# The first FFN's down products with activations stationary, their results turned by VectorE and exchanged by DMA

## The chip, the cores and the metric

The kernel runs on one core of one Trainium2 chip. The metric is the device time of one execution in microseconds (us), as the median of several runs. TensorE does the matrix products, VectorE and ScalarE the elementwise work, GpSimd next to nothing here, and SyncE (SP) issues the DMAs that bring the weights from HBM into SBUF.

## The reference

One layer of a decoder trunk over 256 tokens of width 2048, in float32. Three sublayers each normalise x, shift and scale it by vectors computed from a conditioning vector c (adaLN), and add a gated result:

```python
c_act = silu(c)
sh1, sc1, g1, sh2, sc2, g2, sh3, sc3, g3 = split(c_act @ w_ada + b_ada, 9)
h = rms_norm(x) * (1 + sc1) + sh1
x = x + 0.5 * g1 * ((silu(h @ w1_gate) * (h @ w1_up)) @ w1_down)     # first FFN, hidden width 5632
h = rms_norm(x) * (1 + sc2) + sh2
x = x + g2 * (hybrid_mixer(h) @ w_out)                               # attention and a short convolution
h = rms_norm(x) * (1 + sc3) + sh3
x = x + 0.5 * g3 * ((silu(h @ w2_gate) * (h @ w2_up)) @ w2_down)     # second FFN
```

## The kernel before

**Precision.** Every float32 operand of a large product is split into a high part in TensorE's rounded float32 format and the remainder as a low part. A product is high x high, high x low and low x high. ScalarE makes the high part of a weight (L382), VectorE the low part (L388), right after the weight has landed.

**Entries, halves, ticks.** All weights pass one list of entries, worked off by `run`. An entry is 512 rows by 512 columns (1 MB), loaded by one DMA on SP's queue into one of five raw buffers; the load of the entry four ahead is issued at the start of an entry, so it waits for the buffer of the entry just finished. An entry is consumed in two halves of 256 rows. Four halves are split ahead of the one that TensorE multiplies (`AHEAD`), with five buffers each for high and low parts. After each half the kernel counts one tick; `at(n, fn)` lets `fn` run n ticks after the next one, which puts follow-up work at a chosen place of the instruction streams. Between the FFN's entries stand adaLN entries: 256 or 512 rows of w_ada, multiplied by c and summed by VectorE (L173), one step per 128 rows, summed over partitions at the end.

**Layouts.** x is kept transposed (`xT`: channels on partitions, tokens along the row), as is the normalised input `hS` with its high and low parts. The gate and up products use the activations as stationary operand (`mm_N`: L535, L536, L537): the result has tokens on partitions, and TensorE turns it back with identity matmuls (`flip_split`, L547) into `act`, hidden channels on partitions.

**The down products of the first FFN** use the weights as stationary operand (`group_T`, `mm_T`: L425 and L427). Per 128 rows and 128 output channels one matmul streams 512 columns (256 tokens of high and 256 of low parts) and one 256 columns. The hidden width is done in two groups of channels (six and five blocks of 512); in each, four blocks of 512 output channels, `dg` 0 to 3. A block's results are in four PSUM banks, channels on partitions; `residual` copies them out by ScalarE (L515) and adds them, times the gate, into `xT` by VectorE (L715). After the second group each finished pair of channel blocks is squared for the next norm (`after_residual`). The last 256 channels go by `mm_D` and `fin_one`, straight into the norm.

**The down products of the second FFN** use the activations as stationary operand (`group_R`, again `mm_N`): per 128 rows and 128 tokens three matmuls of 512 columns, results with tokens on partitions, two banks per block.

**The start.** Shift and scale of the first sublayer are needed before anything else, so w_ada comes in eight chunks of 256 channels of each (`ada_chunk`), and the gate and up products of the first FFN run in windows over 256 channels as these become known (`start`, `windows`). A chunk has 16 row blocks, one L173 step each; then eight passes over a matrix of ones (L239) sum over partitions and VectorE and ScalarE make the next part of `hS` (L604, L612, L615). For chunk 0 the row blocks 3, 7 and 11 (`PE_KS`) go to TensorE instead, as one-column matmuls (also L239; a float32 matmul shows as two passes in the trace). The first norm's sums of squares are made by Square on ScalarE and a reduction on VectorE (`first_norm`).

Of the kernel before, what the change touches and what calls it, by code (L numbers as in the profile page):

```python
# [10 lines left out]
F32 = mybir.dt.float32  # L11
# [5 lines left out]
P = 128  # L17
# [19 lines left out]
ATT0 = 4  # L37
QP = 4
ST = 2
DB, DQ, DS, DL, DT = 1, 1, 0, 0, 0  # L40
GT = 3
XT, XD = 8, 3
# [1 line left out]
LAG = 0  # L44
CB = 2
CW = CB * P
PE_KS = (3, 7, 11)
KEEP = 2
LAST = (0, 1, 4, 5, 2, 3, 6, 7, 10, 8, 9)
SET_A = (0, 1, 2, 3, 10)  # L50
# [4 lines left out]
class Kern:  # L55
    def __init__(self, ctx, tc, x, c, w_ada, b_ada, w1_gu, w1_down, w_in, q_norm_w, k_norm_w,
                 conv_w, w_out, w2_gu, w2_down, out):
        self.tc, self.nc = tc, tc.nc
        self.x, self.c, self.out = x[0], c, out[0]
        self.w_ada, self.b_ada = w_ada[0], b_ada  # L60
        self.w1_gu, self.w1_down, self.w2_gu, self.w2_down = w1_gu[0], w1_down[0], w2_gu[0], w2_down[0]
        self.w_in, self.w_out = w_in[0], w_out[0]
        self.qn_w, self.kn_w, self.conv_w = q_norm_w, k_norm_w, conv_w[0]
        pool = lambda name, bufs, **kw: ctx.enter_context(tc.tile_pool(name=name, bufs=bufs, **kw))
        self.const = pool("const", 1)
        self.big = pool("big", 6)
        self.rawp = pool("rawp", NRAW)
        self.hip = pool("hip", AHEAD + 1)
        self.lop = pool("lop", AHEAD + 1)
        self.adap = pool("adap", 1)  # L70
        self.ev = pool("ev", 2)
        self.gatep = pool("gatep", 2)
        self.t2 = pool("t2", NT2)
        self.small = pool("small", 2)
        self.dram = pool("dram", 2, space=bass.MemoryType.DRAM)
        self.psA = pool("psA", 6, space=bass.MemoryType.PSUM)
        self.psM = pool("psM", 2, space=bass.MemoryType.PSUM)
        self.n = 0
        self.later = deque()
        self.soft = deque()  # L80
        self.have = set()
        self.gates = {}
# [148 lines left out]
    def ada_chunk(self, ch):  # L231

        nc = self.nc
        st = {}
        direct = PE_KS if ch == 0 else ()

        def on_pe(w, one, first, last):
            for j in range(4):
# [3 lines left out]
        def make(r):  # L242
            def fn(raw):
                if r == 0:
                    if ch == 0:
                        self.ada_acc = self.adap.tile([P, 2, 512], F32, tag="ada", name=self.nm("ada"))
                    st["acc"] = self.ada_acc[:, ch % 2, :]
                for a in range(4):
                    k = 4 * r + a
                    if k not in direct:  # L250
                        self.soft.append(lambda a=a, k=k: self.ada_step(st["acc"], raw[:, a, :], k))
                for k in range(4 * r, 4 * r + 4):
                    if k in direct:
                        if k == direct[0]:
                            st["ps"] = self.misc()
                        on_pe(raw[:, k % 4, :], self.cact[:, k:k + 1], k == direct[0], False)
            return fn

        def parts(r):
            return lambda raw: [(raw[:, :, CW * s:CW * (s + 1)],  # L260
# [5 lines left out]
        def end():  # L266
            while self.soft:
                self.soft.popleft()()
            if not direct:
                st["ps"] = self.misc()  # L270
            on_pe(st["acc"], self.ones[:, 0:1], not direct, True)
# [257 lines left out]
    def mm_N(self, acc, hi, lo, h, first, last, tts=(0, 1)):  # L529

        nc = self.nc
        for tt in tts:
            ts = slice(tt * P, (tt + 1) * P)
            for kk in range(2):
# [2 lines left out]
                nc.tensor.matmul(acc[tt], h[kk][:, 1, ts], hi[:, kk, :], start=False, stop=last and kk == 1,  # L537
                                 skip_group_check=True)

    def flip_split(self, dst, src):  # L540

        nc = self.nc
# [93 lines left out]
    def first_norm(self):  # L636
# [3 lines left out]
        sq = self.bigt(F32).rearrange("p a b t -> p (a b t)")  # L640
        for i in range(4):
            part = sq[:, 1024 * (i % 2):1024 * (i % 2 + 1)]
            nc.scalar.activation(part, self.xs[i // 2][:, 1024 * (i % 2):1024 * (i % 2 + 1)], AF.Square)
            nc.vector.reduce_sum(self.ssx[:, i:i + 1], part, axis=AX.X)

        def flip(ks, tiles):
            for tt in range(2):
# [55 lines left out]
    def residual_rows(self, dg, tt, acc):  # L703
# [55 lines left out]
    def ffn(self, w_gu, w_down, gate, done, done_last, first):  # L759
# [4 lines left out]
        rows = [512 * u for u in range(4)]  # L764
        act, sil = {}, {}

        def fin_gate(cg):
            def fin(acc):
                sil[cg] = [self.tmp()[:, 0:512] for _ in range(2)]
                for tt in range(2):  # L770
                    nc.scalar.activation(sil[cg][tt], acc[tt], AF.Silu)
            return fin

        def fin_up(cg):
            def fin(acc):
                act[cg] = self.bigt()
                for tt in range(2):
                    nc.vector.tensor_mul(sil[cg][tt], acc[tt], sil[cg][tt])
                self.at(ST, lambda: self.flip_split(act[cg], sil[cg]))
            return fin  # L780

        rhs = lambda k: self.hS[:, k]
# [16 lines left out]
        for gi, (a, b) in enumerate(GROUPS):  # L799
# [6 lines left out]
            for dg in range(4):  # L806
# [392 lines left out]
```

## Time and profile before

| | |
|---|---|
| Median of 3 runs | 1918.27 us (1916.52 to 1919.71) |
| Profiled execution, own time | 1920.87 us |
| Its span | 1919.2 us |
| TensorE busy | 1887.4 us, 98% |
| VectorE busy | 1408.9 us, 73% |
| ScalarE busy | 928.5 us, 48% |
| DMA | 501.79 MB, mean 261 GB/s |

The profile is of one execution. The span runs from the first to the last instruction; what lies around it makes up the difference to the execution's own time. Matmuls are pipelined, so the recorded durations of neighbours overlap, and the distance between starts tells what one costs.

### The profile page before, as it was taken

The numbers are of one execution on the slowest core, as the hardware profiler recorded it, in microseconds if no ns is written. First come the engines' busy times: TensorE is split into PE (matmuls) and PEld (weight loads), VectorE is DVE, ScalarE is ACT, GpSimd is POOL, SyncE is SP. The second block draws the span as 40 slices with busy tenths as digits, with TensorE's granted clock in tenths as the row PEclk, the third lists the DMA queues.
The fourth block names the chain that finished last, engine by engine and source line by source line (L and its number), as shares of the span: only waits on it lengthen the run. The fifth ranks groups of instructions, "written<-read, shape, count | busy, mean of one in ns | idle before, by whom it ended". The sixth has DMA issues, their size and how long they took to land.

```text
span 1919.2 us, 23244 instructions
## 1 busy us (share of the span) xinstructions
PE 1887.4 (98%) x9127; PEld 1585.5 (83%) x9127; DVE 1408.9 (73%) x1614; ACT 928.5 (48%) x1167; POOL 2.0 (0%) x11
## 2 busy tenths in 40 slices
PE   5999999999999999999999999999999999999998
PEld 4888888888888888888888888888888888888887
DVE  7878888788788789787889997667675545554454
ACT  4667784444444444456554454544443334444432
POOL 0000000000000000000000000000000000000000
PEclk8999999999999999999999999999999999999999
DMA  9898988888888878678769885677775556555562
GB/s 363 308 328 311 335 284 307 303 286 324 297 305 310 314 274 313 214 260 284 264 231 328 296 314 190 202 263 269 283 266 210 197 197 197 184 189 193 180 212 73
DMA packets 240678, 501.79 MB, mean 261 GB/s; under 512 B 8430, under 2 KB 43448, under 8 KB 240312
## 3 DMA queue, kind: packets, MB, share of 16 engines
q1 hardware_dynamic: 240536, 500.30, 74.4%
q8 instruction: 71, 1.16, 0.2%
q14 instruction: 39, 0.32, 0.0%
q10 hardware_dynamic: 32, 0.01, 0.0%
HBM read 498.17 MB, written 2.11 MB: 261 GB/s over the span
## 4 chain that ended last, share of the span: by engine, by line
PE 97%; DVE 2%; DMA 1%; ACT 0%; issue 0%; SPq 0%; DVEq 0%
PE acc L535 23%; PE acc L536 23%; PE acc L537 23%; PE acc L425 16%; PE acc L427 8%; DVE ada L173 1%; PE m L547 1%; DMA raw<-in_w_ada_dram 1%; PE acc L437 0%; PE acc L438 0%; PE acc L436 0%; DVE lo L388 0%; PE m L239 0%; PE m L1084 0%; PE m L1061 0%
## 5 line engine op out<-in xcount | busy, mean ns | idle before, releaser
L388 DVE TENSOR_TENSOR lo<-raw,hi 128x1024 fp32r<-128x1024 f32 x656 | 792.6, 1222 | 399.8 <-ACT hi L382 396.6
L382 ACT CAST hi<-raw 128x1024 fp32r<-128x1024 f32 x656 | 685.1, 1052 | 736.5 <-PE acc L537 493.5
L535 PE MATMUL acc<-hi,hS 128*128 128x512 f32 x1600 | 632.5, 395 | 7.3 <-ACT hS L612 7.2
L536 PE MATMUL acc<-lo,hS 128*128 128x512 f32 x1600 | 626.7, 392 | 1.3 <-DVE lo L388 1.3
L537 PE MATMUL acc<-hi,hS 128*128 128x512 f32 x1600 | 626.5, 392 | 0.0
L173 DVE SCALAR_TENSOR_TENSOR ada<-raw,cact,ada 128x1024 f32<-128x1024 f32 (+1 forms) x327 | 357.1, 1092 | 8.4 <-DMA raw<-in_w_ada_dram 1.4
L535 PEld LDWEIGHTS acc<-hi,hS 128*128 128x128 f32 x1600 | 302.8, 189 | 70.1 <-ACT hS L612 8.1
L536 PEld LDWEIGHTS acc<-lo,hS 128*128 128x128 f32 x1600 | 303.0, 189 | 63.6 <-DVE lo L388 2.3
L537 PEld LDWEIGHTS acc<-hi,hS 128*128 128x128 f32 x1600 | 302.5, 189 | 64.1 <-DVE hS L615 0.4
L425 PE MATMUL acc<-big,hi 128*128 128x512 f32 x888 | 315.4, 399 | 0.0
L427 PE MATMUL acc<-big,lo 128*128 128x256 f32 x888 | 249.5, 281 | 0.0
L425 PEld LDWEIGHTS acc<-big,hi 128*128 128x128 f32 x888 | 166.9, 188 | 40.5
L427 PEld LDWEIGHTS acc<-big,lo 128*128 128x128 f32 x888 | 167.9, 189 | 0.1
L535 PE MATMUL acc<-hi,big 128*128 128x512 f32 x352 | 137.2, 390 | 0.0
L536 PE MATMUL acc<-lo,big 128*128 128x512 f32 x352 | 137.0, 389 | 0.0
L537 PE MATMUL acc<-hi,big 128*128 128x512 f32 x352 | 137.0, 389 | 0.0
L425 PE MATMUL acc<-hS,hi 128*128 128x512 f32 x384 | 136.5, 400 | 0.0
L427 PE MATMUL acc<-hS,lo 128*128 128x256 f32 x384 | 107.3, 279 | 0.0
L425 PEld LDWEIGHTS acc<-hS,hi 128*128 128x128 f32 x384 | 72.2, 188 | 16.8
L536 PEld LDWEIGHTS acc<-lo,big 128*128 128x128 f32 x352 | 66.1, 188 | 13.7
L535 PEld LDWEIGHTS acc<-hi,big 128*128 128x128 f32 x352 | 66.1, 188 | 13.7
L537 PEld LDWEIGHTS acc<-hi,big 128*128 128x128 f32 x352 | 66.1, 188 | 13.7
(151 smaller groups left out, 910.6 us busy)
## 6 DMA issues: line engine op xcount, KB each, us to landing
raw<-in_w_gu_dram SPq DMA_DIRECT2D x170, 1024.0 KB, 5.2
raw<-in_w_ada_dram SPq DMA_DIRECT2D x112, 1024.0 KB, 5.2
raw<-in_w_down_dram SPq DMA_DIRECT2D x88, 1024.0 KB, 5.6
raw<-in_w_in_dram SPq DMA_DIRECT2D x48, 1024.0 KB, 7.2
raw<-in_w_ada_dram SPq DMA_DIRECT2D x64, 512.0 KB, 5.6
raw<-in_w_out_dram SPq DMA_DIRECT2D x16, 1024.0 KB, 6.1
raw<-in_w_gu_dram SPq DMA_DIRECT2D x12, 512.0 KB, 5.5
big<-in_x_dram SPq DMA_DIRECT2D x2, 1024.0 KB, 7.0
```

Source lines behind the costliest of these rows:

```text
L173: nc.vector.scalar_tensor_tensor(acc, w, self.cact[:, k:k + 1], acc, op0=ALU.mult, op1=ALU.add)
L382: nc.scalar.copy(hi, raw[:, 2 * h:2 * h + 2, :])
L388: nc.vector.tensor_sub(lo, raw[:, 2 * h:2 * h + 2, :], hi.bitcast(F32))
L425: nc.tensor.matmul(o, hi[:, kk, cs], rhs[kk].rearrange("p a t -> p (a t)"), start=first and kk == 0, stop=False)
L427: nc.tensor.matmul(o[:, 0:T], lo[:, kk, cs], rhs[kk][:, 0, :], start=False, stop=last and kk == 1)
L535: nc.tensor.matmul(acc[tt], h[kk][:, 0, ts], hi[:, kk, :], start=first and kk == 0, stop=False, skip_group_check=True)
L536: nc.tensor.matmul(acc[tt], h[kk][:, 0, ts], lo[:, kk, :], start=False, stop=False, skip_group_check=True)
L537: nc.tensor.matmul(acc[tt], h[kk][:, 1, ts], hi[:, kk, :], start=False, stop=last and kk == 1, skip_group_check=True)
L547: nc.tensor.transpose(ps[:, i * T + tt * P:i * T + (tt + 1) * P], src[tt][:, (2 * pr + i) * P:(2 * pr + i + 1) * P], self.ident)
```

## The change

The down products of the first FFN, except the last 512 output channels after the second group, use `group_R`: activations stationary, results with tokens on partitions in two PSUM banks. `turned` brings them back: VectorE transposes each bank in blocks of 32 x 32 from PSUM into an SBUF tile with the blocks in another order; four ticks after the next one, 16 DMAs on SP's queue, each 32 partitions x 2 x 128 values (32 KB), carry the blocks to their partitions; three ticks later four VectorE operations multiply by the gate and add into `xT`. A pool for one exchanged tile is new. There is also a path that would treat the activations in the same way; `on_pe` returns True always, so it isn't taken.

Two more edits are at the start. `PE_KS` now sends row blocks 3, 7, 11 and 15 of chunk 0 and row blocks 13, 14 and 15 of chunk 1 to TensorE; those of chunk 1 are multiplied when the chunk ends. And the first norm's reduction on VectorE is replaced by the sum that ScalarE's Square can give along with its result.

```diff
+SX, SA = 4, 7
-PE_KS = (3, 7, 11)
+PE_KS = {0: (3, 7, 11, 15), 1: (13, 14, 15)}
+        self.exp = pool("exp", 1)
 ...
-        direct = PE_KS if ch == 0 else ()
+        direct = PE_KS.get(ch, ())
 ...
+                if ch == 0:
+                    rows_on_pe(r, raw)
+                elif r == 3:
+                    st["raw"] = raw
 ...
+        def rows_on_pe(r, raw):
+            for k in range(4 * r, 4 * r + 4):
+                if k in direct:
+                    if k == direct[0]:
+                        st["ps"] = self.misc()
+                    on_pe(raw[:, k % 4, :], self.cact[:, k:k + 1], k == direct[0], False)
 ...
         def end():
             while self.soft:
                 self.soft.popleft()()
+            if ch:
+                rows_on_pe(3, st["raw"])
 ...
+    def exchange(self, tr, fn):
+        st = {}
+        def go():
+            ex = self.exp.tile([P, 2, 512], F32, tag="ex", name=self.nm("ex"))
+            for a in range(4):
+                for c in range(4):
+                    self.nc.sync.dma_start(ex[32 * c:32 * c + 32, :, P * a:P * (a + 1)],
+                                           tr[32 * a:32 * a + 32, :, P * c:P * (c + 1)])
+            st["ex"] = ex.rearrange("p tt (a k j) -> p k (tt a) j", a=4, k=4)
+        self.at(SX, go)
+        self.at(SA, lambda: fn(st["ex"]))
 ...
-            nc.scalar.activation(part, self.xs[i // 2][...], AF.Square)
-            nc.vector.reduce_sum(self.ssx[:, i:i + 1], part, axis=AX.X)
+            nc.scalar.activation(part, self.xs[i // 2][...], AF.Square,
+                                 accum_out=self.ssx[:, i:i + 1])
 ...
+    def turned(self, dg, gate, done):
+        st = {}
+        def add(ex):
+            for k in range(4):
+                d = 4 * dg + k
+                self.want(gate, d // 8)
+                xd = self.xT[:, d, :].rearrange("p (ta j) -> p ta j", j=32)
+                self.nc.vector.scalar_tensor_tensor(xd, ex[:, k], self.mod[:, 16 * gate + d:16 * gate + d + 1], xd,
+                                                    op0=ALU.mult, op1=ALU.add)
+                if done and k % 2:
+                    done(d - 1)
+        def finish(tt, acc):
+            if tt == 0:
+                st["tr"] = self.ev.tile([P, 2, 512], F32, tag="ev", name=self.nm("ev"))
+            self.nc.vector.transpose(st["tr"][:, tt, :].rearrange("p (c k j) -> p c k j", k=4, c=4), self.by_quad(acc))
+            if tt == 1:
+                self.exchange(st["tr"], add)
+        return finish
 ...
-                if first:
-                    down += self.group_T(w_down, urows, 512 * dg, lhs, fin, fin_one if last and dg == 3 else None)
+                if not first:
+                    down += self.group_R(w_down, urows, 512 * dg, lhs, fin_rows)
+                elif last and dg == 3:
+                    down += self.group_T(w_down, urows, 512 * dg, lhs, fin, fin_one)
                 else:
-                    down += self.group_R(w_down, urows, 512 * dg, lhs, fin_rows)
+                    down += self.group_R(w_down, urows, 512 * dg, lhs, self.turned(dg, gate, done if last else None))
```

## Rows read from the trace of the kernel before

**Rows 1.** The page: busy time of the engines; the chain that ended last.

```profile
PE 1887.4 (98%) x9127; PEld 1585.5 (83%) x9127; DVE 1408.9 (73%) x1614; ACT 928.5 (48%) x1167; POOL 2.0 (0%) x11
...
PE 97%; DVE 2%; DMA 1%; ACT 0%; issue 0%; SPq 0%; DVEq 0%
```

**Rows 2.** Timeline of ScalarE, first FFN's down products: start, us, instruction [idle before <-releaser].

```profile
352.44 1.05 ACT L382 CAST hi<-raw 128x1024 fp32r<-128x1024 f32 x1 [1.78 <-PE acc L425]
...
375.04 1.05 ACT L382 CAST hi<-raw 128x1024 fp32r<-128x1024 f32 x1 [1.77 <-PE acc L425]
```

**Rows 3.** Windows: length, busy of PE, PEld, DVE, ACT, POOL, PEclk, DMA share, GB/s.

```profile
311.60:448.50 136.90, 136.90 (x781) 118.99 (x780) 108.08 (x121) 57.01 (x63) 0.00 (x0) 1.00 0.85 302
674.00:787.00 113.00, 113.00 (x684) 100.20 (x683) 91.92 (x117) 50.96 (x62) 0.00 (x0) 1.00 0.81 286
```

**Rows 4.** Timeline of TensorE, the start.

```profile
19.75 1.71 PE L239 MATMUL m<-cact,raw 128*128 128x1 f32 x8
...
42.38 0.39 PE L537 MATMUL acc<-hi,hS 128*128 128x512 f32 x1
47.00 1.58 PE L239 MATMUL m<-ones,ada 128*128 128x1 f32 x8 [4.23 <-DVE ada L173]
48.44 0.77 PE L535 MATMUL acc<-hi,hS 128*128 128x512 f32 x1
...
53.71 0.60 PE L535 MATMUL acc<-hi,hS 128*128 128x512 f32 x1
```

**Rows 5.** Windows of the start, columns as in rows 3.

```profile
16.00:20.00 4.00, 1.24 (x4) 1.09 (x5) 3.80 (x10) 0.01 (x1) 0.00 (x0) 0.58 1.08 388
28.00:47.00 19.00, 13.39 (x49) 10.19 (x48) 18.48 (x23) 7.75 (x12) 0.00 (x0) 0.85 1.07 381
50.00:54.00 4.00, 4.00 (x11) 3.13 (x10) 3.52 (x5) 3.60 (x6) 0.00 (x0) 0.50 0.53 205
```

**Rows 6.** Timeline of ScalarE, second FFN's down products.

```profile
1499.08 1.05 ACT L382 CAST hi<-raw 128x1024 fp32r<-128x1024 f32 x1 [1.67 <-PE acc L537]
...
1512.67 1.05 ACT L382 CAST hi<-raw 128x1024 fp32r<-128x1024 f32 x1 [1.67 <-PE acc L537]
```

**Rows 7.** Groups by line, 311.6 to 447.6 us: busy us, mean ns | idle before.

```profile
L388 DVE TENSOR_TENSOR lo<-raw,hi 128x1024 fp32r<-128x1024 f32 x48 | 58.1, 1222 | 23.8 <-ACT hi L382 23.7
...
L715 DVE SCALAR_TENSOR_TENSOR xT<-ev,mod,xT 128x256 f32<-128x256 f32 x24 | 9.8, 480 | 0.0
L515 ACT COPY ev<-acc 128x512 f32<-128x512 f32 x12 | 6.1, 592 | 0.0
...
L188 DVE STREAM_TRANSPOSE t<-ada 128x512 f32<-128x512 f32 x2 | 1.4, 705 | 0.0
...
L778 DVE TENSOR_TENSOR t<-acc,t 128x512 f32<-128x512 f32 x2 | 1.3, 684 | 0.0
```

**Rows 8.** The raw buffers, 311 to 450 us: issue ns min/median/max; us from issue to landing.

```profile
L352 SPq DMA_DIRECT2D raw<-in_w_down_dram x20: 367/368/368, 312.0 to 423.7; - x20
...
DMA to landing us min/median/max: 5.1/6.7/8.3
```

**Rows 9.** Timeline of SP's queue, at the start and in the first FFN's down products.

```profile
8.26 5.61 SPq L352 DMA_DIRECT2D raw<-in_w_ada_dram  x6
...
347.70 7.19 SPq L352 DMA_DIRECT2D raw<-in_w_down_dram  x2
```

**Rows 10.** Timeline of VectorE, the start.

```profile
15.24 2.33 DVE L173 SCALAR_TENSOR_TENSOR ada<-raw,cact,ada 128x512 f32<-128x512 f32 x3 [1.44 <-DMA raw<-in_w_ada_dram]
...
18.53 5.47 DVE L173 SCALAR_TENSOR_TENSOR ada<-raw,cact,ada 128x512 f32<-128x512 f32 x7
...
43.83 3.11 DVE L173 SCALAR_TENSOR_TENSOR ada<-raw,cact,ada 128x512 f32<-128x512 f32 x4
```

**Rows 11.** The chain that ended last, in order of time: start, us, what.

```profile
78.60 0.79 PE m L239 x8
```

More of the change, by code (lines that the diff above doesn't have):

```diff
@@ L251, in fn @@
                         self.soft.append(lambda a=a, k=k: self.ada_step(st["acc"], raw[:, a, :], k))
[L252 to L256, printed above, removed]
-            return fn
+                if ch == 0:
+                    rows_on_pe(r, raw)
+                elif r == 3:
+                    st["raw"] = raw
+            return fn
+        def rows_on_pe(r, raw):
[4 more added lines that the diff above has]
+                    on_pe(raw[:, k % 4, :], self.cact[:, k:k + 1], k == direct[0], False)
         def parts(r):
@@ L538, in mm_N, with by_quad, quads @@
                                  skip_group_check=True)
+    def by_quad(self, src):
+        return src.rearrange("p (k c j) -> p c k j", k=4, c=4)
+    def quads(self, t):
+        return t.rearrange("p (c k j) -> p c k j", k=4, c=4)
+    def exchange(self, tr, fn):
[9 more added lines that the diff above has]
+        self.at(SA, lambda: fn(st["ex"]))
     def flip_split(self, dst, src):
@@ L642, in first_norm @@
             part = sq[:, 1024 * (i % 2):1024 * (i % 2 + 1)]
-            nc.scalar.activation(part, self.xs[i // 2][:, 1024 * (i % 2):1024 * (i % 2 + 1)], AF.Square)
-            nc.vector.reduce_sum(self.ssx[:, i:i + 1], part, axis=AX.X)
+            nc.scalar.activation(part, self.xs[i // 2][:, 1024 * (i % 2):1024 * (i % 2 + 1)], AF.Square,
+                                 accum_out=self.ssx[:, i:i + 1])
         def flip(ks, tiles):
@@ L765, in ffn, with on_pe @@
         act, sil = {}, {}
+        def on_pe(cg):
+            return True
         def fin_gate(cg):
@@ L770, in fin @@
                 for tt in range(2):
-                    nc.scalar.activation(sil[cg][tt], acc[tt], AF.Silu)
+                    if on_pe(cg):
+                        nc.scalar.activation(sil[cg][tt], acc[tt], AF.Silu)
+                    else:
+                        nc.scalar.activation(self.quads(sil[cg][tt]), self.by_quad(acc[tt]), AF.Silu)
             return fin
@@ L775, in fin, with parts @@
             def fin(acc):
-                act[cg] = self.bigt()
-                for tt in range(2):
-                    nc.vector.tensor_mul(sil[cg][tt], acc[tt], sil[cg][tt])
-                self.at(ST, lambda: self.flip_split(act[cg], sil[cg]))
+                if on_pe(cg):
+                    act[cg] = self.bigt()
+                    for tt in range(2):
+                        nc.vector.tensor_mul(sil[cg][tt], acc[tt], sil[cg][tt])
+                    self.at(ST, lambda: self.flip_split(act[cg], sil[cg]))
+                    return
+                tr = self.ev.tile([P, 2, 512], F32, tag="ev", name=self.nm("ev"))
+                for tt in range(2):
+                    nc.vector.tensor_mul(self.quads(sil[cg][tt]), self.by_quad(acc[tt]), self.quads(sil[cg][tt]))
+                    nc.vector.transpose(tr[:, tt, :], sil[cg][tt])
+                def parts(ex):
+                    act[cg] = self.bigt()
+                    hi, lo = (act[cg][:, :, i, :].rearrange("p k (ta j) -> p k ta j", j=32) for i in range(2))
+                    nc.scalar.copy(hi, ex)
+                    nc.vector.tensor_sub(lo, ex, hi.bitcast(F32))
+                self.exchange(tr, parts)
             return fin
```

## The prediction, made before the changed kernel was run

> **What bounds the kernel now.** I read the page's totals first, then its chain of waits: TensorE is busy for 98% of the span and makes 97% of the chain that ended last [rows 1]. So a change pays through fewer TensorE microseconds in a stage where TensorE is the last to finish, or through idle time of TensorE that goes; VectorE's and ScalarE's work counts only where it makes TensorE late. Next ScalarE's timeline in the stage that changes, the first FFN's down products (some 311 to 448 us for the first group of channels, 674 to 787 us for the second). Each half of a weight entry (two blocks of 128 rows by 512 channels) begins with one cast L382, and each cast there waits for L425 on TensorE [rows 2]: the distance of two casts is TensorE's time for one half. Then the windows of the stage: granted clock 1.00, TensorE without a hole, VectorE 79 to 81% busy, the DMA engines 81 to 85% at 286 to 302 GB/s [rows 3]. Last the start, the only place besides the two later norms where TensorE waits for long: it stands still from 42.8 to 47.0 us for VectorE's L173 [rows 4], and its clock is at half afterwards [rows 5].
>
> **The down products turned round.** Weights stationary, a half is 16 matmuls: eight of 512 columns and eight of 256. Nine casts in a row lie between 352.44 and 375.04 us, so eight halves took 22.60 us, 2.825 us each [rows 2]. Activations stationary, a half is 12 matmuls of 512 columns. The same helper with the same kinds of operands already runs in the second FFN's down products: six casts from 1499.08 to 1512.67 us, 13.59 us for five halves, 2.718 us each [rows 6]. The columns are the same in both (8 x 768 = 12 x 512 = 6144); what goes is four matmuls' fixed part and four weight loads. Turned round are the first group (6 entries x 2 halves x 4 blocks of channels = 48 halves) and three of four blocks of the second (5 x 2 x 3 = 30). 78 x (2.825 - 2.718) = 8.3 us less on TensorE. I take it whole, since the casts wait for TensorE in both places.
>
> A rule speaks against this term: the Trainium skill, "TensorE: Matmul & The Clock Gate", section "Back-to-back issue gap", puts a warm matmul at N/2.4 + 2.5 ns. By it a half would be 8 x (215.8 + 109.2) = 2.600 us before and 12 x 215.8 = 2.590 us after, and the term 0.8 us; the casts show 2.825 and 2.718 us, so the trace does not agree.
>
> **What follows each block.** Before: four evacuations on ScalarE (L515, 592 ns) and eight residual operations on VectorE (L715, 480 ns), 2.4 and 3.8 us per block of channels. After: two block transposes on VectorE straight out of PSUM and four residual operations. A transpose in SBUF took 705 ns, a VectorE operation of the same size that reads PSUM (L778) 684 ns; I take 0.70 us, between 0.68 and 1.22 us (L388, twice the columns), and 0.48 us for the residual with its new strides, at most 0.69 us (L778, twice the columns) [rows 7]. Per block VectorE has 2 x 0.70 + 4 x 0.48 = 3.3 us in place of 3.8 (worst 5.2), ScalarE 2.4 us less. Both are hidden by TensorE: VectorE has (136.9 - 108.1)/48 = 0.6 us free per half [rows 3], 6 to 7 us per block. A transpose waits for TensorE's last matmuls with the next low parts (L388) queued behind it; four halves are prepared by then, so TensorE doesn't notice.
>
> **The exchange.** Per block 16 DMAs of 32 KB on SP's queue, 7 x 16 = 112 in all, issued four ticks after the block's end and used three ticks later. One issue takes 0.37 us in this stage [rows 8]; at the start, with the DMA engines full, six took 5.61 us, 0.94 each [rows 9]. I take 0.37 (the row of the same stage): 16 x 0.37 = 5.9 us of SP; the far end is 15.0 us. A load, 32 times the bytes of a piece, lands 5.1 to 8.3 us after its issue here [rows 8], so the last piece is there 5.9 + 5.1 = 11.0 to 5.9 + 8.3 = 14.2 us after the first issue. The cover: three ticks of 2.72 us until VectorE wants it, and some three halves still prepared for TensorE when VectorE stops, together 16.3 us. So I cost it at nothing; if the cover goes, L388 is late next, then TensorE. What is queued behind the 16 on SP are weight loads: 5.9 us later at most, often less, since SP sits between two loads waiting for a buffer (two issues of 0.37 us fill a stretch of 7.19 us at 347.70) [rows 9]. A raw buffer comes round every five entries, some three of them weights of 5.4 us (the others adaLN rows), 16 us; landing (6.7) and splitting (about 5.4) take 12 of them, so 4 us are spare, and the prepared halves lend 8 more. The bytes, 0.5 MB at some 300 GB/s, are 1.7 us per 27 us of engines that are 81 to 85% busy. Nothing below zero is to be had here: neither engine relieved is late.
>
> A second rule speaks against this: the Trainium skill, "DMA: Bandwidth & Descriptors", section "Rules for kernel authors", wants many small transfers merged, since under 64 KB one pays mostly overhead. Sixteen in series at the 2.0 us of that page's fit (made for GpSimd's DMAs) would be an estimated 32 us per block; no row before shows pieces this small.
>
> **The start.** Row block 15 of chunk 0 goes from VectorE to TensorE: one of the seven L173 of 18.53 us, 5.47/7 = 0.78 us [rows 10]. TensorE's eight extra passes (1.71 us for eight at half clock) run behind those of 19.75 us, to 23.2 us [rows 4], while VectorE ends at 24.0 - 0.8 = 23.2 us: 0.8 us earlier from there on, for up to 47.0 us VectorE is the bound, 97% busy from 28 us on [rows 5]. Row blocks 13 to 15 of chunk 1 go too: three of the four L173 of 43.83 us, 2.3 us [rows 10], so VectorE's sum is done at 47.0 - 0.8 - 2.3 = 43.9 us. TensorE, free at 42.8 - 0.8 = 42.0 us, now has 24 passes, 0.79 us for eight at full clock [rows 11], to 44.4 us, then the eight of the old sum, to 45.2 us where the profile has 48.6 us (47.00 and 1.58 [rows 4]): 3.4 us. From 48.44 to 53.71 us twelve matmuls took 5.27 us [rows 4] at a granted clock of 0.50, the 1.2 GHz level [rows 5], after a stretch of 4 us in which TensorE did nothing; at the upper level (2.4 GHz) they take 12 x 2.718/12 = 2.7 us [rows 6]. With that stretch filled I expect the upper level to hold: 2.6 us. Between the ends of 0 (one-column passes do no better than standing still: from 16 to 20 us, with TensorE 1.24 us busy, the clock fell to 0.58 on average [rows 5]) and 2.6 I take 2.6, as the hole is filled end to end, with dense matmuls on both sides. The sums of squares that ScalarE's Square now makes itself save four VectorE reductions; VectorE then stands waiting for a load until 15.24 us anyway [rows 10]: nothing.
>
> **Sum.** 8.3 + 3.4 + 2.6 = 14.3 us off the profiled execution: span 1919.2, own time 1920.87 us, so 1906.6. That execution lies 2.6 us above the median of the runs (1918.27); against the median, 1904.0 us.
>
> **Rivals.**
> 1. The clock falls all the same behind the one-column passes. For: the window from 16 to 20 us. Against: a gap of only 3.2 us between dense matmuls. 8.3 + 3.4 = 11.7 us, 1906.6 us.
> 2. The start is bound by transfers: the DMA engines move 381 GB/s, 1.07 of their time, from 28 to 47 us, and what VectorE gives up is waited for at the next load. Against: from 50 to 54 us they move only 205 GB/s, the loads had caught up [rows 5]. 8.3 alone, 1910.0 us.
> 3. A half costs its columns alone: 6144 in both, so the turn is worth nothing on TensorE and 3.4 + 2.6 = 6.0 us remain, 1912.3 us. Against: [rows 2, 6]. The first rule above comes to nearly the same.
> 4. The exchange shows in part, 1 us of TensorE per block (landing at the far end and a VectorE that catches up slowly): 7 us back, 1911.0 us; at 2 us per block the gain is gone.
> 5. The slower side: SP issues the small DMAs at the loaded price of 0.94 us. 15.0 + 6.7 to landing is 21.7 us against a cover of 16.3: TensorE stands 5.4 us per block, 7 x 5.4 = 38 us, 1942 us. It decides from 2.0 us per block on, that is from 0.73 us per issue. For: DMA engines at 85%. Against: the loads of this very stage issue in 0.37 us.
>
> **Chances.** Forecast 0.50, rival 1 0.15, rival 2 0.10, rival 3 0.03, rival 4 0.12 (half of it within 0.2%), rival 5 0.10. A measurement of this kernel tells about 0.2%, 3.8 us, from no change. Faster: 0.50 + 0.15 + 0.10 + 0.03 + 0.06 = 0.84; same 0.06; slower 0.10. The range goes from 1899 (the runs before spread over 3.2 us, and the turned blocks may free a further wait) to 1915 us, which leaves out rival 5 and half of rival 4.
>
> **What would show it.** Turned halves: casts 2.72 us apart in the first FFN's down products. Exchange: TensorE without holes there, SP's issues near 0.37 us, VectorE waiting for the exchanged tile a few us at most. Start: the first L535 after chunk 1's sum near 45 us, granted clock 1.00 in the windows after it. Wrong would be holes behind L388 in the first FFN's down stages, or a clock of 0.50 after 45 us.

## The result: 1% slower, and the profile after

The changed kernel took 1938.53 us (median of 4 runs, 1937.32 to 1940.27), the kernel before 1918.99 us beside it: ratio 1.010, interval 1.0088 to 1.0112. Forecast were 1904.0 us and a range up to 1915; the time lies on the side to which the prediction gave 0.10. In the kernel after, the low part's subtraction is L398, the cast L392, the weights-stationary pair L435/L437, the activations-stationary matmuls L545 to L547, chunk products L241, the exchange DMA L566, the residual that reads it L752.

The page first, the same two lines as in [rows 1]:

```profile
PE 1888.6 (97%) x8847; PEld 1575.8 (81%) x8847; DVE 1397.2 (72%) x1592; ACT 914.0 (47%) x1143; POOL 2.0 (0%) x11
...
PE 86%; DMA 5%; DVE 5%; SPq 2%; ACT 1%; issue 1%; DVEq 0%; ACTq 0%
```

TensorE's share of the chain that ended last fell from 97% to 86%; DMAs, VectorE and, new, SP's queue make up the rest. The windows of the two down stages and of the join behind the second, columns as in [rows 3]:

```profile
311.50:454.60 143.10, 135.22 (x590) 110.73 (x590) 106.08 (x114) 50.30 (x50) 0.00 (x0) 0.98 0.80 286
677.30:796.10 118.80, 114.75 (x573) 97.72 (x571) 86.78 (x99) 41.16 (x43) 0.00 (x0) 0.97 0.75 264
796.10:811.70 15.60, 3.90 (x12) 2.87 (x11) 9.36 (x21) 6.33 (x12) 0.00 (x0) 0.77 0.57 208
```

Before, TensorE was busy without a hole in both stages; now it stands for 7.9 us of the first and 4.1 us of the second, and for 11.7 us of the join. On TensorE's timelines the first down stage grew from 137.1 to 143.1 us, and the stretch from the second's first matmul to the mixer's first from 119.9 to 134.4 us. These are +6.0 and +14.5 us; the start gave back 0.2 and the second FFN's gate-up, untouched, ran 1.4 us shorter: +18.9 of the 19.0 us between the spans (1919.2 and 1938.2). The longest holes, on TensorE's timeline:

```profile
448.42 0.79 PE L546 MATMUL acc<-lo,big 128*128 128x512 f32 x1 [6.01 <-DVE lo L398]
...
767.86 0.58 PE L437 MATMUL acc<-big,lo 128*128 128x256 f32 x1 [4.02 <-DVE lo L398]
...
804.91 1.22 PE L803 MATMUL m<-ssq,ones 128*128 128x256 f32 x2 [8.78 <-DVE ssq L790]
```

Two are holes behind the low parts, which the prediction had named as the sign that it is wrong. The waits in the first down stage (waiting engine and line, for what: us in total, times, longest) say why the low parts are late; the first line is of the kernel before, the others are of the kernel after:

```profile
ACT hi L382 <- PE acc L425: 77.2, 43, 3.2
```

```profile
ACT hi L392 <- DMA raw<-in_w_down_dram: 41.7, 11, 11.6
...
DVE xT L752 <- DMA ex<-ev: 18.1, 3, 8.6
...
ACT hi L392 <- DMA raw<-in_w_gu_dram: 14.3, 2, 13.7
```

Casts wait for weights, where before they waited for TensorE and never for a load, and VectorE waits for the exchanged tile. SP's queue shows where the weights are. Its timeline around the third block, where three lines follow one another:

```profile
428.70 0.37 SPq L362 DMA_DIRECT2D raw<-in_w_ada_dram  x1
429.11 13.62 SPq L566 DMA_DIRECT2D ex<-ev  x16
442.84 1.07 SPq L362 DMA_DIRECT2D raw<-in_w_gu_dram  x2
```

For 13.6 us no load is issued. The view of the exchange tile gives the price of a piece (issue, ns min/median/max), and SP's own waits give the rest of the burst:

```profile
L566 SPq DMA_DIRECT2D ex<-ev x112: 585/595/1452, 353.0 to 796.1; - x112
...
  DMA ex<-ev: 42.3, 7
```

```profile
SPq L566 <- DMA raw<-in_w_ada_dram: 14.6, 7, 3.3
...
SPq L566 <- DMA raw<-in_w_gu_dram: 2.5, 1, 2.5
```

A piece takes 0.595 us where a 1 MB load takes 0.37. And pieces wait for weight loads with whose data they have nothing to do: the DMAs of SP's queue use eight completion semaphores in turn, and in the three of these waits for which the trace has the landing of the DMA eight issues earlier, the piece began 0.02 us after it (the piece at 437.03 after the load issued at 428.70, landed 437.02). The seven bursts last 11.0 to 15.0 us.

At the start, TensorE, ScalarE and the windows:

```profile
38.66 0.50 PE L545 MATMUL acc<-hi,hS 128*128 128x512 f32 x1 [2.39 <-ACT big L959]
...
45.85 2.73 PE L241 MATMUL m<-cact,raw 128*128 128x1 f32 x24
48.44 1.03 PE L241 MATMUL m<-ones,ada 128*128 128x1 f32 x8
49.33 0.49 PE L545 MATMUL acc<-hi,hS 128*128 128x512 f32 x1
```

```profile
37.08 1.04 ACT L392 CAST hi<-raw 128x1024 fp32r<-128x1024 f32 x1 [7.07 <-DMA raw<-in_w_gu_dram]
```

```profile
39.80:43.20 3.40, 3.40 (x10) 2.62 (x9) 3.36 (x4) 1.70 (x4) 0.00 (x0) 0.50 1.07 379
...
50.10:53.50 3.40, 3.40 (x9) 2.63 (x8) 2.77 (x6) 3.27 (x5) 0.00 (x0) 0.50 0.80 299
```

The first L535 of chunk 1, at 48.44 us before [rows 4], is L545 at 49.33 us, not 45.2. A cast waits 7.07 us for a gate-up load, the PSUM copies queue behind it on ScalarE, TensorE stands 2.39 us, and the clock is at 0.50 (1.2 GHz) twice for 3.4 us.

### The profile page after: what moved, and what is told of

Same layout as the page of the kernel before. It is cut to its first block, busy times and chain, and to the rows that moved or that the text cites. A ratio compares the mean times of both kernels' runs of the same rounds, so it can differ in the third digit from the quotient of the medians.

```text
span 1938.2 us, 22730 instructions
## 1 busy us (share of the span) xinstructions
PE 1888.6 (97%) x8847; PEld 1575.8 (81%) x8847; DVE 1397.2 (72%) x1592; ACT 914.0 (47%) x1143; POOL 2.0 (0%) x11
## 4 chain that ended last, share of the span: by engine, by line
PE 86%; DMA 5%; DVE 5%; SPq 2%; ACT 1%; issue 1%; DVEq 0%; ACTq 0%
PE acc L545 24%; PE acc L546 24%; PE acc L547 24%; PE acc L435 7%; PE acc L437 4%; DMA raw<-in_w_ada_dram 3%; DVE lo L398 2%; DVE ada L175 2%; SPq L566 2%; DMA raw<-in_w_down_dram 1%; PE m L579 1%; DMA raw<-in_w_gu_dram 1%; ACT hi L392 1%; PE m L241 0%; DMA ex<-ev 0%
## 5 line engine op out<-in xcount | busy, mean ns | idle before, releaser
L398 DVE TENSOR_TENSOR lo<-raw,hi 128x1024 fp32r<-128x1024 f32 x656 | 791.5, 1222 | 386.8 <-ACT hi L392 383.9
L392 ACT CAST hi<-raw 128x1024 fp32r<-128x1024 f32 x656 | 683.3, 1053 | 768.7 <-PE acc L547 523.0
L545 PE MATMUL acc<-hi,hS 128*128 128x512 f32 x1600 | 631.3, 395 | 10.3 <-ACT hS L644 7.9
L547 PE MATMUL acc<-hi,hS 128*128 128x512 f32 x1600 | 625.9, 391 | 0.0
L545 PEld LDWEIGHTS acc<-hi,hS 128*128 128x128 f32 x1600 | 302.1, 189 | 73.0 <-ACT hS L644 9.3
L547 PEld LDWEIGHTS acc<-hi,hS 128*128 128x128 f32 x1600 | 301.8, 189 | 64.5 <-DVE hS L647 0.9
L546 PE MATMUL acc<-lo,big 128*128 128x512 f32 x664 | 259.9, 391 | 7.9 <-DVE lo L398 7.8
L545 PE MATMUL acc<-hi,big 128*128 128x512 f32 x664 | 259.8, 391 | 0.0
L547 PE MATMUL acc<-hi,big 128*128 128x512 f32 x664 | 259.2, 390 | 0.0
L546 PEld LDWEIGHTS acc<-lo,big 128*128 128x128 f32 x664 | 125.2, 189 | 35.5 <-DVE lo L398 9.8
L545 PEld LDWEIGHTS acc<-hi,big 128*128 128x128 f32 x664 | 125.1, 188 | 26.2
L547 PEld LDWEIGHTS acc<-hi,big 128*128 128x128 f32 x664 | 125.2, 189 | 25.7
L435 PE MATMUL acc<-hS,hi 128*128 128x512 f32 x384 | 136.5, 399 | 0.0
L437 PE MATMUL acc<-hS,lo 128*128 128x256 f32 x384 | 107.3, 279 | 0.0
L435 PE MATMUL acc<-big,hi 128*128 128x512 f32 x264 | 95.4, 403 | 0.0
L435 PEld LDWEIGHTS acc<-hS,hi 128*128 128x128 f32 x384 | 72.1, 188 | 16.8
L437 PE MATMUL acc<-big,lo 128*128 128x256 f32 x264 | 75.0, 284 | 4.0 <-DVE lo L398 4.0
L437 PEld LDWEIGHTS acc<-hS,lo 128*128 128x128 f32 x384 | 72.4, 189 | 0.0
L435 PEld LDWEIGHTS acc<-big,hi 128*128 128x128 f32 x264 | 50.4, 191 | 11.7
```

The lines of the kernel that those rows point to most:

```text
L392: nc.scalar.copy(hi, raw[:, 2 * h:2 * h + 2, :])
L398: nc.vector.tensor_sub(lo, raw[:, 2 * h:2 * h + 2, :], hi.bitcast(F32))
L435: nc.tensor.matmul(o, hi[:, kk, cs], rhs[kk].rearrange("p a t -> p (a t)"), start=first and kk == 0, stop=False)
L437: nc.tensor.matmul(o[:, 0:T], lo[:, kk, cs], rhs[kk][:, 0, :], start=False, stop=last and kk == 1)
L545: nc.tensor.matmul(acc[tt], h[kk][:, 0, ts], hi[:, kk, :], start=first and kk == 0, stop=False, skip_group_check=True)
L546: nc.tensor.matmul(acc[tt], h[kk][:, 0, ts], lo[:, kk, :], start=False, stop=False, skip_group_check=True)
```

## Experiments

The theories. **Q**: the burst of pieces holds up SP's queue, so the loads are late. **S**: the start is bound by its loads and loses its clock behind the one-column passes. Rivals for the down stages: **P**, 512-byte runs hold up the DMA engines; **V**, VectorE's transposes hold up the low parts; **W**, VectorE's wait for the exchanged tile alone. Times are medians with the ratio to the kernel before on the same chip (1919.2 to 1919.6 us there).

### The two halves of the change

`e1_start_only` keeps the start edits and has the down products as before; `e2_down_only` the other way round.

```diff
 # e1: the old branch of the down products
+if first: down += self.group_T(w_down, urows, 512 * dg, lhs, fin, ...)
 # e2
-PE_KS = {0: (3, 7, 11, 15), 1: (13, 14, 15)}
+PE_KS = {0: (3, 7, 11)}          # and reduce_sum in place of accum_out
```

> The edits of the start alone; the first FFN's down products as before the change (weights stationary, no exchange). Theory S: the start is bound by its loads and by the clock that falls behind one-column passes, so these edits are worth next to nothing: 0 +- 2 us against the kernel before, and a granted clock of 0.50 for one stretch after chunk 1's sum. Rival (the forecast): 3.4 to 6.0 us faster, 1912 to 1915.

> The turned down products with their exchange alone; the start as before the change. Theory Q (SP's queue: 16 pieces of 0.6 us each, from the ninth on each waiting for the landing of the DMA eight issues earlier, so that no weight load is issued for 10 to 14 us): all of the loss is here, 18 to 20 us slower than before, 1937 to 1939. Rival: the start's edits, by shifting the loads, carry part of it: 1925 to 1932.

e1: 1917.36 us, 0.9993 (0.9984 to 1.0003). e2: 1942.77 us, 1.0126 (1.011 to 1.0142). The whole loss is in the down products; the start is worth 0 to 3 us, not 6.0. One trace is too few to see a gain of that size: in the nine traces with the start as before the first stage ends between 309.1 and 311.9 us, in the four with the edited start (e1, the changed kernel, and e8 and f7 below) between 310.0 and 311.7. e2 came out above the 1937 to 1939 us that I expected, and 4.2 us above the changed kernel, which is more than the start gives in its traces; the intervals of the two overlap by a hair, and why stays open. TensorE's timeline and the windows of e1:

```profile
43.06 2.73 PE L241 MATMUL m<-cact,raw 128*128 128x1 f32 x24
45.66 1.79 PE L241 MATMUL m<-ones,ada 128*128 128x1 f32 x8
47.31 0.77 PE L545 MATMUL acc<-hi,hS 128*128 128x512 f32 x1
```

```profile
42.00:45.60 3.60, 3.60 (x30) 3.40 (x28) 1.85 (x3) 1.08 (x2) 0.00 (x0) 1.00 1.03 376
45.70:49.00 3.30, 3.30 (x13) 3.01 (x14) 1.34 (x5) 0.80 (x2) 0.00 (x0) 0.51 1.02 354
```

TensorE is busy throughout, with no hole from 37.5 us on, and the clock goes to 1.2 GHz at 45.7 us all the same, right behind the 24 one-column passes. That is the prediction's rival 1.

### The exchange taken away, or issued for nobody

`e3_no_exchange` issues no exchange DMA, and the residual reads the transposed tile itself (the output's blocks are in other places). `e4_unused_exchange` issues them all, and the residual reads the transposed tile too. Both with the start as before.

```diff
 def go():
-    ex = self.exp.tile(...)                                    # e3; e4 keeps the tile and the DMAs
-    ... self.nc.sync.dma_start(ex[...], tr[...])               # e3; sixteen of them
-    st["ex"] = ex.rearrange(...)                               # both
+    st["ex"] = tr.rearrange(...)                               # both
```

> As the down products alone, but without the 112 DMAs: the residual reads the transposed tile directly, so its blocks are added at the wrong places. Theory Q, and rival P (pieces of 512 bytes slow the DMA engines): 8 us faster than before (78 halves at 2.718 in place of 2.825 us), 1910 to 1911, no hole of TensorE in the down stages. Rival V (VectorE, which now waits for TensorE at the transposes and holds up the low parts): still slower than before, 1922 or more.

> As the down products alone, with all 112 DMAs issued, but the residual reads the transposed tile directly (blocks at the wrong places) and nobody waits for the exchanged tile. Theory Q: the weight loads behind the pieces are as late as before, so the first down stage stays at 141 to 144 us (137.1 before the change), while the wait in front of the next norm goes back to some 5 us: 1922 to 1927. Rival W (VectorE's own wait for the exchanged tile is what makes TensorE late): 8 us faster than before, 1910 to 1911.

e3: 1913.08 us, 0.9969 (0.9959 to 0.9979). e4: 1930.15 us, 1.0054 (1.0036 to 1.0072). Windows of e3's down stages and its join on TensorE's timeline, then waits of e4 from 306 to 460 us:

```profile
311.20:443.40 132.20, 132.20 (x590) 109.59 (x589) 107.01 (x115) 51.63 (x50) 0.00 (x0) 1.00 0.86 308
666.00:777.70 111.70, 111.70 (x573) 95.49 (x572) 91.06 (x110) 46.58 (x50) 0.00 (x0) 1.00 0.84 298
```

```profile
779.08 0.70 PE L798 MATMUL m<-ssq,ones 128*128 128x256 f32 x2 [1.34 <-DVE ssq L785]
```

```profile
ACT hi L392 <- DMA raw<-in_w_down_dram: 39.1, 10, 12.8
...
ACT hi L392 <- DMA raw<-in_w_gu_dram: 18.1, 3, 14.1
```

e3 has the transposes and all of the turned matmuls, and no hole: V falls. The stages are 5.0 and 3.1 us shorter than before (137.1 to 132.1, 114.8 to 111.7), and 1.6 us of that is lost at the join, where the norm waits 1.34 us for VectorE; so the time is 2 us above the 1910 to 1911 that I expected. The changed kernel's 590 matmuls of the first stage took 135.22 us where e3's take 132.20: behind the hole that ends at 448.42 us the granted clock was 0.50 up to 452.8 us, so the holes cost about 3 us more there than their 7.9. In e4 nobody waits for the exchange, and the casts wait for weights about as long as in the changed kernel: late loads cost 1930.15 - 1913.08 = 17 us by themselves (e4's four runs lie between 1926 and 1935 us, above the 1922 to 1927 that I expected), and by difference the 12.6 us from there to e2 are put down to VectorE's wait. W alone is not it, P is not yet excluded.

### The same bytes in other issues

Four kernels, start as before. `e5_spread`: four pieces a step from step 1 to 4. `e6_through_dram`: one write to DRAM and four reads with the same 512-byte runs. `e7_gpsimd_queue`: the sixteen pieces on GpSimd's queue, from step 1. `e10_eight_pieces`: eight pieces of 64 partitions at step 4 (blocks misplaced).

```diff
+for a in range(4): self.at(1 + a, lambda a=a: go(a))                       # e5
+self.nc.sync.dma_start(st["d"].rearrange(...), tr.rearrange(...))          # e6, step 1; st["d"] is in DRAM
+... self.nc.sync.dma_start(ex[32 * c:32 * c + 32], st["d"][:, :, :, c]...) # e6, step 4, four; use at 8
+self.nc.gpsimd.dma_start(ex[...], tr[...])                                 # e7
+self.nc.sync.dma_start(ex[64 * h:64 * h + 64, ...], tr[64 * (a // 2):...]) # e10
```

> Down change alone, start as before; the sixteen pieces of a block are issued four at a time over four steps of the loop (steps 1 to 4 instead of all at step 4), so that weight loads are issued between them. Theory Q (the burst holds up SP's queue: 0.6 us a piece, and from the ninth piece on the wait for the DMA eight issues earlier): a group of four is 2.4 us, no load waits longer, the pieces land 2 steps before their use; 1912 to 1918 us, first down stage 132 to 135 us. Rival P (512-byte runs occupy the DMA engines, so the loads are late however the pieces are issued): like the down change alone, 1936 to 1943 us, stage 140 to 143. If the semaphores of eight DMAs bind also in fours (a piece then waits for a 1 MB load): 1920 to 1930.

> Down change alone, start as before; the exchange goes through DRAM: one write of the transposed block (128 partitions, 4 KB each) at step 1, four reads of 32 partitions with the same 512-byte runs at step 4, use at step 8. Five issues instead of sixteen, the write's and the reads' bytes together twice the exchange's. Theory Q: no burst, 1912 to 1917 us, first down stage 132 to 134 us. Rival P (small runs and bytes occupy the DMA engines): the pieces' loss stays, 1928 to 1940 us.

> Down change alone, start as before; the same sixteen pieces are issued on GpSimd's queue, from step 1. Theory Q (SP's queue): the loads are issued on time, 1912 to 1920 us, first down stage 132 to 136 us; if a piece takes 1 us or more to issue there, the block of 16 to 20 us still ends before its use at step 7, or VectorE waits a few us at the blocks' ends (up to 1925). Rival P (DMA engines held by the pieces): 1928 to 1943 us.

> Down change alone, start as before; the exchange is made in eight pieces of 64 partitions instead of sixteen of 32, all at step 4: the same bytes in the same 512-byte runs, blocks land in other places than they should. It divides theory Q. If a burst is long because a ninth piece waits for the DMA eight issues earlier, eight pieces do not wait: bursts of about 5 us, 1913 to 1919 us. If it is the issue price alone (0.6 us a piece), half the loss of the down change is left: 1926 to 1930. If the price of an issue grows with its runs (1.2 us a piece), bursts of 9.5 us and 1925 to 1935. Rival P: as the down change alone, 1936 to 1943.

e5: 1926.89 us, 1.0039 (1.0026 to 1.0052). e6: 1913.02, 0.9968 (0.9955 to 0.9981). e7: 1913.14, 0.9965 (0.9951 to 0.9979). e10: 1912.77, 0.997 (0.996 to 0.998). Three of the four cost no more than no exchange at all (1913.08). So P falls: the same runs, or twice the bytes (e6), move beside the loads for nothing. e5, e6 and e7 also begin at an earlier step; e10 does not, and is as fast as the faster two, so the earlier step is not what frees the loads. The windows of the third burst's place say the same as to P, the changed kernel first, e7 second (with eight pieces on GpSimd's queue in it); where the DMA engines should have been held up, they had less to do (0.64 against 0.94):

```profile
425.00:448.00 23.00, 17.41 (x77) 14.08 (x75) 13.09 (x14) 4.85 (x6) 0.00 (x0) 0.96 0.64 218
```

```profile
425.00:448.00 23.00, 23.00 (x103) 19.04 (x102) 18.92 (x20) 9.47 (x9) 3.98 (x8) 1.00 0.94 343
```

SP's timeline of e10, then of e5, and e5's waits on SP:

```profile
421.89 7.95 SPq L567 DMA_DIRECT2D ex<-ev  x8
...
450.77 10.22 SPq L567 DMA_DIRECT2D ex<-ev  x8
```

```profile
416.32 7.52 SPq L567 DMA_DIRECT2D ex<-ev  x8
...
425.30 8.20 SPq L567 DMA_DIRECT2D ex<-ev  x8
```

```profile
SPq L567 <- DMA raw<-in_w_ada_dram: 23.4, 11, 3.4
SPq L567 <- DMA raw<-in_w_down_dram: 6.6, 8, 2.4
```

e10's bursts, 6.2 to 10.2 us, were longer than the 5 us expected (in the one at 421.89 us the eighth piece waits for the load just ahead of the burst), and they are still free: the first stage is as long as e3's (132.1 us). Bursts of 11.0 to 15.0 us are not. Its pieces waited for earlier DMAs longer than those of the changed kernel (20.3 us in 8 waits, 17.1 in 8 there), so what made room is half the number of issues. e5 missed my expectation of 1912 to 1918: spreading makes more pieces wait for a load eight issues earlier (30.0 us in 19 waits for the two kinds of load shown), and the third block then holds SP for two stretches of 7.5 and 8.2 us, with loads between them. It was the case named last in its expectation, 1920 to 1930. e7's pieces take less on GpSimd, and wait there for one another with no weight load behind them:

```profile
L566 POOL DMA_DIRECT2D ex<-ev x112: 533/533/674, 346.0 to 760.2; - x112
```

The Trainium skill, "DMA: Bandwidth & Descriptors", "Rules for kernel authors", says that spreading DMAs over the issuing engines gives no bandwidth and saves only issue time at the sequencer. e7 agrees: the bytes are the same, and the time for which the pieces held SP's queue was the whole loss (1913.14 us, 1913.08 without an exchange).

`e11_one_run` asks what the 0.6 us are for: one run of 1 KB per partition in place of two of 512 bytes (blocks misplaced).

```diff
+flat = [t.rearrange("p tt m -> p (tt m)") for t in (ex, tr)]
+self.nc.sync.dma_start(flat[0][32 * c:32 * c + 32, 256 * a:256 * (a + 1)],
+                       flat[1][32 * a:32 * a + 32, 256 * c:256 * (c + 1)])
```

> Down change alone, start as before; sixteen pieces of 32 partitions at step 4 as in the change, but each piece takes one run of 1 KB per partition instead of two of 512 bytes, blocks land in other places than they should. It asks what an issue's 0.6 us is for. If the price goes by runs (64 a piece): about 0.3 to 0.4 us a piece, bursts of 6 to 9 us, 1912 to 1920 us. If it is a fixed price of a transfer of this kind: 0.6 us, bursts of 11 to 15 us, 1936 to 1943 us, as the down change alone.

1939.85 us, 1.0105 (1.0091 to 1.0119), and an issue is as long:

```profile
L567 SPq DMA_DIRECT2D ex<-ev x112: 507/589/1262, 350.5 to 794.3; - x112
```

The price does not go by runs. Nor by partitions: e10's pieces, 64 of them, took 0.607 us. What sets it stays open.

### The start: loads, or the clock

`e8_start_lean` is e1 with chunk 1's row blocks 4 to 11 loaded to a quarter (1.5 MB less; the steps reuse the loaded block, so its sums are others). `e9_start_wide` is e8 with chunk 1's row blocks 13 to 15 multiplied by 128 moving columns (of ones, so its sums are others too).

```diff
+if lean(r): return lambda raw: [(raw[:, 0, ...], self.w_ada[512*r:512*r + P, ...]) ...]             # e8, e9
+on_pe(raw[:, k % 4, :], self.ones if ch else self.cact[:, k:k + 1], ...)  # [128 x 128] operand: e9
```

> Start edits alone, down products as before; of chunk 1's modulation weights row blocks 4 to 11 are loaded to a quarter (1.5 MB less; the steps use the one block that is loaded), so that the second gate-up loads come earlier. Theory S for the loads (the start edits gain little because the loads of 20 to 43 us run at 380 to 396 GB/s): 1.5 MB at 388 GB/s is 3.9 us, the cast's wait of 6.1 us falls to about 2, TensorE's hole of 1.7 us at 37.5 us is gone, VectorE's last step of chunk 1 ends 1.5 us earlier or more, first stage ends 1.5 to 3 us before the 310.5 of the start edits alone; 1913 to 1917 us. Rival (VectorE's own sequence ends last, not a load): the hole goes, chunk 1's sum stays at 45.5 us or so, the stage ends within 0.5 us of the start edits alone.

> As the lean start, and chunk 1's last three row blocks are multiplied with 128 moving columns instead of one (the sums are wrong). Theory S for the clock (it falls because one-column passes do not count as work for TensorE's clock, however close they stand): the half-clock stretch of 6.8 us behind the twelve wider passes starts later, after fewer us, or does not occur; if it is gone the first stage ends up to 3.4 us before the lean start's, less what the wider passes take longer. Rival (the wait for chunk 1's sum behind the passes is what the clock falls for): the half-clock stretch stays, and the stage ends as with the lean start or 0.5 to 1 us later.

e8: 1917.43 us, 0.9983 (0.9973 to 0.9992). e9: 1913.86 us, 0.9973 (0.9962 to 0.9984). TensorE's timelines, e8 and then e9, and the window of 46 to 50 us in each:

```profile
42.66 2.73 PE L241 MATMUL m<-cact,raw 128*128 128x1 f32 x24
...
46.91 0.77 PE L551 MATMUL acc<-hi,hS 128*128 128x512 f32 x1
```

```profile
41.38 2.84 PE L242 MATMUL m<-ones,raw 128*128 128x128 f32 x24
44.05 0.96 PE L242 MATMUL m<-ones,ada 128*128 128x1 f32 x8
44.88 0.48 PE L552 MATMUL acc<-hi,hS 128*128 128x512 f32 x1
```

```profile
46.00:50.00 4.00, 4.00 (x12) 3.37 (x13) 2.29 (x7) 2.20 (x4) 0.00 (x0) 0.50 1.00 338
```

```profile
46.00:50.00 4.00, 4.00 (x20) 3.29 (x19) 3.36 (x6) 4.00 (x7) 0.00 (x0) 1.00 1.04 374
```

In e8 the hole at 37.5 us went with the bytes, and the first stage ended at 310.1 us where e1 has 310.5, a difference inside the spread above (in this run the clock also came back from half later, at 35.1 us, in e1 at 32.1). Over the runs the two take the same time (1917.43 and 1917.36 us), not the 1913 to 1917 of theory S: no gain from fewer loads shows, and I was wrong on that half. The other half held: at the same loads, wider passes in the same place (all 24 of the group) kept the clock at 1.00, and the stage ended at 305.6 us. Of these 4.5 us, 1.3 were there before the passes began (41.38 against 42.66 us) and are not theirs.

### Versions that beat both kernels

`f7_gpsimd_and_start` is the whole change with the pieces on GpSimd's queue. `f10_wide_one` adds the wide passes to it with right values and all loads: 128 moving columns, of which the first holds the value and the others are not read. `f12_wide_both` does the same for chunk 0's passes.

```diff
-self.nc.sync.dma_start(ex[...], tr[...])                                  # f7, from step 1
+self.nc.gpsimd.dma_start(ex[...], tr[...])
-on_pe(raw[:, k % 4, :], self.cact[:, k:k + 1], k == direct[0], False)      # f10: W = 128 for chunk 1
+on_pe(raw[:, k % 4, :], self.cact[:, k:k + W], k == direct[0], False)      # f12: for chunk 0 too
```

> The whole change (start and down products) with the sixteen pieces on GpSimd's queue from step 1: a version to beat both kernels. Theory Q: the down stages as with that queue alone (first 132.1, second 111.7 us, no holes) and the start as in the kernel with the start edits alone (ends 0 to 1.5 us earlier than before): 1909 to 1913 us. If the start's loads and the down stages disturb each other, 1914 to 1919.

> The whole change with the pieces on GpSimd's queue, and chunk 1's last three row blocks multiplied with 128 moving columns (the first holds the values, the others are not read; all loads in full). If the wide passes hold the clock here too: granted clock 1.00 from 42 to 54 us, the half-clock stretch of 6.8 us gone, first stage ends 3 to 4.5 us before the 310.0 of the version without them; 1908 to 1910 us. If the clock stayed in the wide start because of the 1.5 MB that it did not load: the half-clock stretch is back, 1912 to 1913 us.

> As the version before it, and chunk 0's four row blocks as well with 128 moving columns, in passes that stand apart (12.7 to 23.4 us, with holes of 1 to 3 us for loads). If wide passes hold the clock wherever they stand: the half-clock stretch of 17 to 20 us from about 15 us on is shorter or gone, and the gate-up's first matmuls (from 26.6 us) run 0.23 us apart instead of 0.43: up to 3.5 us more, 1904 to 1907 us. If the holes there decide: no change against the version before, 1908 to 1910 us, or 0.5 us more for the wider passes.

f7: 1912.52 us, 0.996 (0.9948 to 0.9973). f10: 1910.23 us, 0.9951 (0.9938 to 0.9965). f12: 1912.26 us, 0.9957 (0.9945 to 0.997). The windows of f7, then of f10, then of f12:

```profile
46.00:50.00 4.00, 4.00 (x14) 3.42 (x14) 1.97 (x7) 1.89 (x4) 0.00 (x0) 0.50 1.05 364
```

```profile
46.00:50.00 4.00, 4.00 (x19) 3.28 (x19) 3.24 (x8) 3.17 (x5) 0.00 (x0) 1.00 1.08 399
```

```profile
28.00:34.00 6.00, 6.00 (x14) 4.74 (x15) 5.89 (x8) 1.05 (x1) 0.00 (x0) 0.50 1.08 390
```

The clock stays up in f10 with all loads in full, so it was not e9's missing bytes. The first stage ends at 306.7 us (f7: 310.0), with the passes begun at nearly the same time (42.45 and 42.57 us); in the three traces with wide passes (e9, f10, f12) it ends between 305.6 and 306.7 us, ahead of all thirteen others. The three intervals overlap, so of the times I only say that all three beat both kernels; that f10's wide passes pay is read from the stage. f12's do nothing for chunk 0: the clock is at half there as before, among passes that stand apart; its median is 2 us above the 1908 to 1910 that I expected for this case.

## Why the prediction was wrong, step by step

- **Down products turned round, 8.3 us: right.** e3 shows 5.0 us for 48 halves and 3.1 us for 30, 0.104 us a half where 0.107 was forecast; the changed kernel's own casts, where nothing holds them up, are 2.72 us apart:

```profile
326.50 1.06 ACT L392 CAST hi<-raw 128x1024 fp32r<-128x1024 f32 x1 [1.67 <-PE acc L547]
...
340.10 1.05 ACT L392 CAST hi<-raw 128x1024 fp32r<-128x1024 f32 x1 [1.67 <-PE acc L547]
```

  Rival 3 falls with it. The formula that the prediction set against this term (the Trainium skill, "TensorE: Matmul & The Clock Gate", section "Back-to-back issue gap") is given there for a matmul by itself, and here each comes with a weight load; its 0.8 us is not what e3 shows (8.1 us in the two stages). The time gained 6.2 us (1919.28 to 1913.08) and not 8.3: the join behind the last block took 1.6 back, which the prediction had not looked at.
- **What follows each block: right.** A transpose out of PSUM took 0.69 us (0.70 forecast), a residual operation 0.48, and e3 has no hole.
- **The exchange, costed at nothing: wrong, and most of the miss** (29.7 us, e2 against e3; 14.3 us of gain were forecast and 19.5 lost, 33.8 in all, and the rest is the start and the join). Its failed step is "I take 0.37 (the row of the same stage)". The row was that of another kind of DMA: a piece takes 0.595 us, with the step to the next 0.64. A second term was not in the sum at all: an issue that waits until the DMA eight issues earlier has landed. So SP was held for 13.6 us in the third burst in place of 5.9, 0.85 us a piece (13.1 us on average over the seven, of which 10.2 are sixteen steps of 0.64 and 2.4 these waits). The cover for the loads (4 us spare and 8 lent by the prepared halves) was judged about right: the runs put the edge between 10.2 us (e10's longest burst, free) and the changed kernel's 11.0 to 15.0. VectorE's wait then adds to it, since the late low parts stand behind L752: 42.3 us in 7 waits, where the prediction wanted to see a few us at most. One term was too high: a piece landed 1.9 us after its issue (median), not the 5.1 to 8.3 us of a load.
- **Rival 5 is what happened, for another reason.** It gave 1942 us from 0.94 us a piece and was to decide from 0.73; 0.85 was measured, and the down change alone took 1942.8. That the times agree so well is luck: the rival's sum counts the start's 6.0 us and 38 us for the exchange. It blamed loaded DMA engines, which in fact had less to do than before, and its evidence against (loads of this stage issue in 0.37 us) was the same wrong row. Nor was 0.94 a price alone: in the trace before, SP's own waits from 0 to 15 us have

```profile
SPq L352 <- DMA raw<-in_w_ada_dram: 1.9, 2, 0.9
```

  and both lie among the six loads of [rows 9], each a wait for the DMA issued eight earlier; without them a load there took 0.62 us. The missing term stood in the row that was read. The second rule that the prediction weighed (the Trainium skill, "DMA: Bandwidth & Descriptors", "Rules for kernel authors", on merging transfers under 64 KB) pointed the right way. One piece did take about 2 us, 1.9 from issue to landing, but sixteen do not add up in series: the step from issue to issue is 0.64 us, and pieces of 64 KB took as long to issue.
- **The start, 6.0 us: 0 to 3.** VectorE's part was right: in e1 its last step ends at 43.85 us, 43.9 forecast. TensorE reached the passes at 43.06 instead of 42.0, after a hole of 1.72 us at 37.5 us, then took 2.73 us for 24 instead of 2.4, and the sum's eight passes ran at half clock: 1.1 us earlier, not 3.4. The 2.6 us for the clock failed as rival 1 said: filling the hole with one-column passes did not keep it. Rival 2 (transfers) explains the hole, not the loss: without it (e8) the kernel took the same time. In the changed kernel the same start gained 0.2 us, with a hole of 2.39 us and two falls of the clock.

## What to carry to other kernels

Price a DMA's issue by a row of the same kind of DMA, and where there is none take the far end: sixteen small pieces on a queue that feeds the loads are a stretch of that queue, to be held against what the loads can be late by, the waits inside the queue included. Put such pieces on a queue with nothing behind them, or merge them until the stretch fits. Spreading them between loads, the obvious mend, made each wait for more loads.

## What was not expected of the hardware

- An issue of 32 KB took 0.595 us on SP, of 64 KB 0.607, with runs of 1 KB 0.589, and 0.533 on GpSimd; a 1 MB load takes 0.37.
- A DMA of SP's queue waits for the completion semaphore of the one eight issues earlier, with no data between them (7 waits for adaLN loads, 14.6 us; longest 3.3 us). Whether the chip asks for this or only the program as compiled, no run here shows.
- TensorE, busy without a hole, fell to 1.2 GHz behind 24 one-column passes in a row (e1, e8); with these 24 passes 128 columns wide it stayed at 2.4 GHz (e9, f10, f12).
